# An encoder layer on one core: value product copied in halves, one filler matmul moved ahead of each head's first scores, transposes of x spread over a pass

## The chip, the cores and the metric

The kernel runs on one core of one Trainium2 chip. The metric is device time in microseconds (us) of one launch, as the median of several runs. The profile shows one execution of the same program, engine by engine: PE (matmul), PEld (PE's weight loads), DVE, ACT, POOL, and SP, which issues the DMAs.

## What is computed

One layer with two token mixers and a gated feed-forward network, for x of 1024 tokens by 1024 channels, all in float32. Branch A is the banded softmax attention, branch B the stick-breaking attention. Cut to what matters:

```python
h = x @ w_in[l]
qa, ka, va, qb, kb, vb, ga, gb = jnp.split(h, split_pts, axis=-1)
y_a = chunk_band_attention(heads_a(qa), heads_a(ka), heads_a(va), rel_bias[l]) @ w_proj_a[l]
y_b = stick_breaking_attention(heads_b(qb), heads_b(kb), heads_b(vb)) @ w_proj_b[l]
gate_a = jax.nn.sigmoid(ga + b_gate[l, :D])
gate_b = jax.nn.sigmoid(gb + b_gate[l, D:])
mix = (gate_a * y_a + gate_b * y_b) @ w_out[l]
x = layer_norm(DEEPNORM_ALPHA * x + mix, ln1_g[l], ln1_b[l])
gu = x @ w_ffn_in[l]
g, u = jnp.split(gu, 2, axis=-1)
ffn = (jax.nn.silu(g) * u) @ w_ffn_out[l]
x = layer_norm(DEEPNORM_ALPHA * x + ffn, ln2_g[l], ln2_b[l])
# chunk_band_attention, per head of 64 channels; a query sees its own chunk of 64 tokens and the 8 before it
scores = q @ k.T / 8 + rel_bias[clip(distance)];  out = softmax(scores) @ v
```

Each branch has eight heads of 64 channels.

## The kernel before

Every float32 product is made from two parts per operand: a rounded high part (fp32r) that ACT casts, and the rest, which DVE gets by subtracting (`split`). A product is then three matmuls (high·high, high·low, low·high), or two where the second operand is stacked on the partitions. The program runs as stages in this order: input projections, the attention of branch A (eight heads), that of branch B (eight heads), branch projections and gates, the output projection with the first layer norm, the feed-forward network. Some large products use a seven-product scheme on quarters of the matrices (`pair_steps`); the steps here do not need it.

**A head of branch A.** Queries come in eight blocks of 128 (b = 0 to 7). `soft_block` makes one block: two or four matmuls into a PSUM bank with the tag "sc" (L695, L696), DVE's custom instruction L738 that adds the bias and takes a running minimum into `st`, ACT's exponential L744, DVE's reciprocal and POOL's scaling L749. `value_steps` then works in two groups g of four query blocks (512 columns). For each block of keys kb, `turn` transposes the weights on PE (L807, into a bank with the tag "tr") and splits them into `pt` (ACT cast L110, DVE subtraction L111); `mult` adds two matmuls, high and low part (L820, L821), into one PSUM bank `pv` of 512 columns. There is one such bank. The order of key blocks is 4, 5, 6, 7, 3, 2, 1, 0 in the first group (g = 0) and 7, 6, 5, 4 in the second (g = 1). In the first group kb = 1 touches columns 0 to 255 and kb = 0 columns 0 to 127 alone; in the second, kb = 5 and kb = 4 do the same. After the last pair ACT copies the bank's 512 columns to `yt` or `yv` (L839), a DMA moves half of the rows, and POOL adds (L843).

**Fillers.** PE is given other matmuls between those of a head: the products of the gates (`gps`, L598), three for each of eight weight blocks, and later those of the first projection. A counter `goal` rises with each step of a head and `fill_until(goal)` takes matmuls from the generator until the counter is met.

**The order around the change.** The loop at the end of the attention part is a list of 12 steps per head. `LEAD` says how many blocks of scores are issued by each step; at the step with position 2 the first block of the *next* head is issued (`LEAD[0][2]` is 9, one more than a head's eight). `pend` holds products back by `LAG` = 2 steps. A scheduler then orders each engine's instructions by priority and data; the rows under "The change" show what comes out.

**The output projection.** It has eight tiles of 128 tokens (`tt`); tiles 4 to 7 are made in plain form, in two passes, hf = 0 for the columns 0 to 511 and hf = 1 for the columns 512 to 1023, 24 matmuls per tile and pass (`ops`, L117, L118, L120). DVE adds each to `acc` (`take_in`, L1322); in the second pass `norm_1` follows for each tile. The feed-forward network wants the normed x transposed: `x1_operands(0, ...)` transposes tiles 0 to 3 (already normed) in pairs kt, kt + 4 (four transposes each, L1178, into "tr" banks), splits each into `x1A` (ACT cast, DVE subtraction) and keeps an unsplit copy `x1raw` (ACT, L1188). There are three "tr" banks. All four pairs are issued after tile 4 of the second pass.

Of the kernel before, what the change touches and what calls it, by code (L numbers as in the profile page):

```python
# [18 lines left out]
P = 128  # L19
# [11 lines left out]
HW = 512  # L31
# [17 lines left out]
def hybrid_trunk_kernel(ctx: ExitStack, tc, x, xt, w_first, w_v, w_in, b_gate, rel_bias, w_proj,  # L49
# [6 lines left out]
    nc = tc.nc  # L56
# [7 lines left out]
    def slot(tag, name, dtype=F32):  # L64
        return pool.tile([P, 1024], dtype, tag=tag, name=name, bufs=SLOTS[tag])
# [16 lines left out]
    mm = nc.tensor.matmul  # L82
# [208 lines left out]
    for j in range(4):  # L291
        cs = (LO, HI)[j % 2]
# [495 lines left out]
    def value_steps(hd, g, wt):  # L788

        br, h = hd["br"], hd["h"]  # L790
        reach = (4, 8)[br]
        q0 = 4 * g
        nm = f"{'ab'[br]}{hd['n']}_{g}"
        pv = []

        kbs = [4, 5, 6, 7, 3, 2, 1, 0] if g == 0 else [7, 6, 5, 4]
        steps = []
        for i, kb in enumerate(kbs):
            lo_q = max(q0, kb - reach)
            hi_q = min(q0 + 3, kb)  # L800
            n = (hi_q - lo_q + 1) * P
            pts = []

            def turn(kb=kb, lo_q=lo_q, hi_q=hi_q, n=n, pts=pts):
                tp = bank("tr", f"tp_{nm}_{kb}")
                for qb in range(lo_q, hi_q + 1):
                    tr(tp[:, (qb - lo_q) * P:(qb - lo_q + 1) * P],  # L807
                       wt[qb - q0][:, (kb - qb) * P:(kb - qb + 1) * P], ident)
                pt = slot("pt", f"pt_{nm}_{kb}", F32R)
                split(pt[:, 0:n], pt[:, HW:HW + n], tp[:, 0:n])  # L810
                pts.append(pt)

            def mult(i=i, kb=kb, lo_q=lo_q, n=n, pts=pts):
                v = hd["v"]
                if i == 0:
                    pv.append(bank("pv", f"pv_{nm}"))
                last = i == len(kbs) - 1
                cs = slice((lo_q - q0) * P, (lo_q - q0) * P + n)
                pt = pts[0]
                mm(pv[0][:, cs], v[:, kb, :], pt[:, 0:n], start=(i == 0), stop=False)  # L820
                mm(pv[0][:, cs], v[:, kb, :], pt[:, HW:HW + n], start=False, stop=last)  # L821
                if last:
                    yt = hd["yt"]()
                    r = slice(h * DH, (h + 1) * DH)
                    gs = slice(g * HW, (g + 1) * HW)
                    if hd["i"] == 7:
                        nc.scalar.copy(yt[r, gs], pv[0][DH:P])
                        nc.vector.tensor_tensor(yt[r, gs], pv[0][0:DH], yt[r, gs], ALU.add)
                        if h == 1:
                            if g == 0:  # L830
                                yh[7], yl[7] = (slot("xt", f"y{p}7", F32R) for p in "hl")
                            split(yh[7][:, gs], yl[7][:, gs], yt[:, gs])
                    else:

                        if g == 0:
                            hd["yv"] = slot("yt", f"yv_{nm}")
                        yv = hd["yv"]
                        both, other = (yt, yv) if h == 0 else (yv, yt)
                        nc.scalar.copy(both[:, gs], pv[0])  # L839
                        dma(other[r, gs], both[(DH, 0)[h]:(P, DH)[h], gs])  # L840

                        def add():
                            nc.gpsimd.tensor_tensor(yt[r, gs], yt[r, gs], yv[r, gs], ALU.add)  # L843
                            if h == 1 and g == 1:
                                if hd["i"] > 4:
                                    for n, cs in ((6, LO), (8, HI)):
                                        later.append([n, lambda cs=cs: split_y(hd["i"], yt, cs)])
                                else:
                                    dma(y_dr[hd["i"]], yt)
                        later.append([3 + hd["br"], add])  # L850

            steps.append((turn, mult))
        return steps

# [96 lines left out]
    def fill_until(t):  # L951
        while state["t"] < t and not state["done"]:
            try:
                state["t"] += next(fill)
            except StopIteration:
                state["done"] = True
# [44 lines left out]
    goal = 0.0  # L1001
# [4 lines left out]
    for si, (hd, g, st, box) in enumerate(vsteps):  # L1006
        hidx, pos = si // nhead, si % nhead
# [13 lines left out]
        early = hd["br"] == 0 and st == LAG - 1 and len(pend) == LAG  # L1021
        if early and g == 1:
            pend.pop(0)()
        while wi < min(hidx * 8 + LEAD[hd["br"]][pos], len(wunits)):
            wunits[wi]()
            wi += 1
# [13 lines left out]
        last = goal  # L1040
# [18 lines left out]
    acc_t = []  # L1059
# [38 lines left out]
    for n, c in enumerate((6, 7, 5, 4, 2, 3, 1, 0)):  # L1098
# [25 lines left out]
        else:  # L1124
            g = m_first[c - 4]
# [42 lines left out]
    ops_1 = {p: [] for p in range(1, 8)}  # L1168
    x1raw, x1low, ops_21 = [], [], []

    def x1_operands(hf, acc_t):

        for kt in range(4):
            tps = []
            for k in (kt, kt + 4):
                tp = bank("tr", f"x1ps{hf}_{k}")
# [50 lines left out]
    def left_f(f):  # L1227
        prep_left(Wf[f], f"f{f}", w_ffn_in[f], "bw" if f == 2 else "op")
# [139 lines left out]
    for hf, cs in enumerate((LO, HI)):  # L1368
        for tt in range(4, 8):
# [17 lines left out]
                    right_f(1)  # L1387
            if hf == 1:
                norm_1(tt)
                if tt == 4:  # L1390
                    x1_operands(0, acc_t)
        if hf == 0:
            left_f(2)

    first_h = []

# [177 lines left out]
```

## Time and profile before

| what | us |
|---|---|
| runs of the kernel before | 1424.55, 1424.86, 1427.96 (median 1424.86) |
| the profiled execution, own time | 1425.8 |
| its span | 1424.0 |
| branch A's attention in the trace | about 342.5 to 475 |
| one of its heads | about 15.7 |
| output projection's plain tiles | about 735 to 775 |

The profiled execution took 1425.8 us by its own time, 0.9 us more than the median of the runs, and its span is 1.8 us shorter than that. The trace gives for every instruction its start, its length and, where its engine was idle ahead of it, the idle time with the event that ended it. Matmuls overlap one another in the records, so on PE the distance from start to start counts and not the length. PEld rows are weight loads; a wait of a matmul for data shows there first.

### The profile page before, as it was taken

The numbers are of one execution on the slowest core, as the hardware profiler recorded it, in microseconds if no ns is written. First come the engines' busy times: TensorE is split into PE (matmuls) and PEld (weight loads), VectorE is DVE, ScalarE is ACT, GpSimd is POOL, SyncE is SP. The second block draws the span as 40 slices with busy tenths as digits, with TensorE's granted clock in tenths as the row PEclk, the third lists the DMA queues.
The fourth block names the chain that finished last, engine by engine and source line by source line (L and its number), as shares of the span: only waits on it lengthen the run. The fifth ranks groups of instructions, "written<-read, shape, count | busy, mean of one in ns | idle before, by whom it ended". The sixth has DMA issues, their size and how long they took to land.

```text
span 1424.0 us, 19039 instructions
## 1 busy us (share of the span) xinstructions
PE 1412.3 (99%) x6672; PEld 1172.8 (82%) x6672; DVE 1054.5 (74%) x1669; ACT 683.0 (48%) x1188; POOL 245.9 (17%) x313
## 2 busy tenths in 40 slices
PE   9999999999999999999999999999999999999997
PEld 7888888888888888888888888888888888888886
DVE  8866657635777778878988947776777656978767
ACT  6444444555778788774423624444444433212201
POOL 0000000002555779750001000000000000100014
PEclk9999999999999999999999999999999999999999
DMA  7486478856676468755651224443444458787602
GB/s 255 159 295 223 163 251 311 294 183 212 213 222 199 135 228 296 249 196 198 231 198 69 74 75 163 148 148 135 150 159 163 148 192 280 281 312 238 204 15 104
DMA packets 104974, 276.54 MB, mean 194 GB/s; under 512 B 10400, under 2 KB 26784, under 8 KB 104880
## 3 DMA queue, kind: packets, MB, share of 16 engines
q1 hardware_dynamic: 104880, 275.35, 55.9%
q8 instruction: 52, 0.85, 0.3%
q14 instruction: 42, 0.34, 0.1%
HBM read 179.33 MB, written 92.30 MB: 191 GB/s over the span
## 4 chain that ended last, share of the span: by engine, by line
PE 93%; DVE 4%; ACT 2%; issue 1%; DMA 0%; POOL 0%; DVEq 0%; ACTq 0%; SPq 0%
PE sxf L180 16%; PE sxp L180 9%; PE szf L180 8%; PE dx L1496 6%; PE v L482 5%; PE szp L180 5%; PE gps L598 4%; PE syf L180 4%; PE dz L1496 3%; PE yAps L896 3%; PE syp L180 2%; PE tp_b L807 2%; PE ops L1343 2%; PE tp_a L807 2%; PE plain L348 2%; PE fpswh_h L118 2%
## 5 line engine op out<-in xcount | busy, mean ns | idle before, releaser
L784 POOL TENSOR_TENSOR w_b<-w_b,kp_b 128x511 f32<-128x511 f32 (+3 forms) x96 | 96.1, 1017 | 24.9 <-DVE kp_b L779 17.1
L1452 POOL TENSOR_TENSOR wdyt<-wdyt 128x512 f32<-128x512 f32 x8 | 11.2, 1405 | 512.5 <-DVE wdgt L1451 492.0
L779 DVE TENSOR_TENSOR_SCAN kp_b<-kp_b,ident_ps 128x512 f32<-128x512 f32 (+2 forms) x64 | 56.5, 884 | 23.3 <-ACT kp_b L776 22.4
L776 ACT ACTIVATE kp_b<-sc_b 128x512 f32<-128x512 f32 (+3 forms) x96 | 48.4, 505 | 30.7 <-PE sc_b L696 27.4
L180 PE MATMUL szf<-x1S63h,wcf 128*128 128x512 f32 x168 | 55.1, 389 | 0.0
L111 DVE TENSOR_TENSOR pt_b<-tp_b,pt_b 128x512 fp32r<-128x512 f32 (+1 forms) x96 | 50.0, 544 | 6.9 <-ACT pt_b L110 6.3
L719 POOL MEMSET bias<- 64x64 f32 x2 | 0.3, 144 | 313.4 <-ACT bias L715 313.4
L1427 DVE TENSOR_TENSOR x<-dx,x 128x512 f32<-128x512 f32 x64 | 43.3, 685 | 14.7 <-PE dx L1496 14.6
L111 DVE TENSOR_TENSOR sl<-h,sl 128x512 fp32r<-128x512 f32 x56 | 38.3, 685 | 19.5 <-ACT sl L110 19.5
L749 POOL TENSOR_SCALAR w_a<-w_a,st_a 128x640 f32<-128x640 f32 (+2 forms) x64 | 42.3, 666 | 57.3 <-PE sc_a L696 23.8
L110 ACT CAST sl<-h 128x512 fp32r<-128x512 f32 x56 | 34.7, 619 | 35.3 <-PE syf L180 17.1
L110 ACT CAST pt_b<-tp_b 128x512 fp32r<-128x512 f32 (+1 forms) x96 | 47.5, 505 | 8.0 <-PE tp_b L807 7.6
L744 ACT ACTIVATE w_a<-w_a,st_a 128x640 f32<-128x640 f32 (+2 forms) x64 | 44.8, 702 | 13.5 <-DVE st_a L738 12.2
L1156 POOL TENSOR_TENSOR mv<-mv,neghalf 128x1 f32<-128x1 f32 x16 | 11.9, 744 | 222.1 <-DVE mv L1155 222.0
L1274 ACT ACTIVATE h<-sxf 128x512 f32<-128x512 f32 x21 | 12.5, 597 | 77.3 <-PE sxf L180 77.3
L777 ACT ACTIVATE w_b<-sc_b 128x511 f32<-128x511 f32 (+3 forms) x96 | 48.6, 506 | 0.0
L111 DVE TENSOR_TENSOR pt_a<-tp_a,pt_a 128x512 fp32r<-128x512 f32 (+1 forms) x96 | 44.9, 485 | 4.8 <-ACT pt_a L110 3.1
L807 PE MATMUL tp_b<-ident,w_b 128*128 128x128 f32 x288 | 47.8, 273 | 0.4 <-DVE pt_b L111 0.3
L110 ACT CAST pt_a<-tp_a 128x512 fp32r<-128x512 f32 (+1 forms) x96 | 39.1, 432 | 11.0 <-PE tp_a L807 10.8
L807 PE MATMUL tp_a<-ident,w_a 128*128 128x128 f32 x240 | 43.2, 275 | 1.0 <-POOL w_a L749 0.4
L807 PEld LDWEIGHTS tp_b<-ident,w_b 128*128 128x128 f32 x288 | 35.6, 140 | 9.6 <-PE sc_b L696 1.3
L598 PE MATMUL gps<-xl,wh_g 128*128 128x512 f32 x96 | 43.0, 448 | 0.0
(1787 smaller groups left out, 4814.3 us busy)
## 6 DMA issues: line engine op xcount, KB each, us to landing
s_dr<-sl SPq DMA_DIRECT2D x112, 256.0 KB, 2.3
sd<-s_dr SPq DMA_DIRECT2D x56, 512.0 KB, 4.7
wLf<-in_w_ffn_in_dram SPq DMA_DIRECT2D x22, 512.0 KB, 4.5
wRf<-in_w_ffn_in_dram SPq DMA_DIRECT2D x22, 512.0 KB, 3.6
v_dr<-vc SPq DMA_DIRECT2D x16, 512.0 KB, 3.2
qs<-q_dr SPq DMA_DIRECT2D x16, 512.0 KB, 6.9
kh<-k_dr SPq DMA_DIRECT2D x16, 512.0 KB, 6.1
kl<-k_dr SPq DMA_DIRECT2D x16, 512.0 KB, 6.9
```

The lines of the kernel that those rows point to most:

```text
L110: return (nc.scalar.copy(dst_h, src), nc.vector.tensor_tensor(dst_l, src, dst_h.bitcast(F32), ALU.subtract))
L111: nc.vector.tensor_tensor(dst_l, src, dst_h.bitcast(F32), ALU.subtract))
L180: mm(acc, lw[:, ks], rx, start=(first and kt == i == 0), stop=(kt == 3 and i == 2), skip_group_check=not first)
L482: mm(accs[j], a, b, start=(first and kt == n == 0), stop=(kt == 3 and n == 2), skip_group_check=True)
L598: mm(acc[hf], lw[:, ks], rx[k][:, (LO, HI)[hf]], start=(k == j == 0), stop=(k == KT - 1 and j == 2))
L744: nc.scalar.activation(s[:, 0:w], s[:, 0:w], AF.Exp, bias=st[:, m:m + 1], scale=-1.0, accum_out=st[:, 2:3])
L776: nc.scalar.activation(kp[:, c0:e], sc[:, 0:n], AF.Sigmoid, scale=-1.0)
L777: nc.scalar.activation(be[:, m0:e], sc[:, m0 - c0:n], AF.Sigmoid)
L779: nc.vector.tensor_tensor_scan(kp[:, 0:e], kp[:, 0:e], ident_ps()[:, 0:e], 0.0, ALU.mult, ALU.add)
L784: nc.gpsimd.tensor_tensor(be[:, m0:e], be[:, m0:e], kp[:, m0 - 1:e - 1], ALU.mult)
L807: tr(tp[:, (qb - lo_q) * P:(qb - lo_q + 1) * P], wt[qb - q0][:, (kb - qb) * P:(kb - qb + 1) * P], ident)
L1496: mm(acc, a, b, start=(first and i == n == 0), stop=(i == n - 1 == 1), skip_group_check=not first)
```

## The change

It has three parts.

First, in branch A the bank `pv` is copied in two pieces. The columns 256 to 511 are copied after the pair that precedes the last two (kb = 2 in the first group, kb = 6 in the second), and the columns 0 to 255 after the last pair. The tile `yv` is taken at the first copy.

Second, at position 2 of a step list of branch A, `fill_until(goal + 0.5)` takes one filler before the scores of that step are issued.

Third, `x1_operands(0, ...)` takes a list of pairs: pair 0 is issued after the first pass (after `left_f(2)`), pairs 1 and 2 after tile 4 of the second pass, and pair 3 after tile 5.

```diff
+        def copy_out(part):
+            yt = hd["yt"]()
+            if "yv" not in hd:
+                hd["yv"] = slot("yt", f"yv_{nm}")
+            both, other = (yt, hd["yv"]) if h == 0 else (hd["yv"], yt)
+            nc.scalar.copy(both[:, g * HW:(g + 1) * HW][:, part], pv[0][:, part])
+            return both, other
...
-                mm(pv[0][:, cs], v[:, kb, :], pt[:, 0:n], start=(i == 0), stop=False)
-                mm(pv[0][:, cs], v[:, kb, :], pt[:, HW:HW + n], start=False, stop=last)
+                two = br == 0
+                done = two and i == len(kbs) - 3
+                mm(pv[0][:, cs], v[:, kb, :], pt[:, 0:n], start=(i == 0), stop=False,
+                   skip_group_check=two)
+                mm(pv[0][:, cs], v[:, kb, :], pt[:, HW:HW + n], start=False, stop=last or done,
+                   skip_group_check=two)
+                if done:
+                    copy_out(slice(2 * P, HW))
...
-                        if g == 0:
-                            hd["yv"] = slot("yt", f"yv_{nm}")
+                        both, other = copy_out(slice(0, 2 * P if two else HW))
                         yv = hd["yv"]
-                        both, other = (yt, yv) if h == 0 else (yv, yt)
-                        nc.scalar.copy(both[:, gs], pv[0])
...
+        if hd["br"] == 0 and pos == 2:
+            fill_until(goal + 0.5)
         while wi < min(hidx * 8 + LEAD[hd["br"]][pos], len(wunits)):
...
-    def x1_operands(hf, acc_t):
+    def x1_operands(hf, acc_t, kts=range(4)):
-        for kt in range(4):
+        for kt in kts:
...
                 norm_1(tt)
-                if tt == 4:
-                    x1_operands(0, acc_t)
+                if tt < 6:
+                    x1_operands(0, acc_t, ((1, 2), (3,))[tt - 4])
         if hf == 0:
             left_f(2)
+            x1_operands(0, acc_t, (0,))
```

The number of matmuls is the same; ACT has 16 instructions more (two copies of 256 columns for each one of 512). In the changed file L807 becomes L815, L820 and L821 become L830 and L832, the copy is L801, L1178 becomes L1191 and L1188 becomes L1201.

On ACT, in the third head of branch A from the cast of key block 0 of its first group to the exponential of block 5 (w_a and st_a: a block's weights and sums; pt_a_0_x and pt_a_1_x: split weights of key block x in group 0 and 1; bias: the next heads' bias tile), there stands before:

```order
L110 CAST pt_a_0_0_3397<-tp_a_0_0_3395 128x128
L110 CAST pt_a_1_7_3428<-tp_a_1_7_3423 128x512
L744 ACTIVATE w_a_0_3_3297,st_a_3_3411<-w_a_0_3_3297,st_a_3_3411 128x640
L839 COPY yt_3437<-pv_a_0_3330 128x512
L110 CAST pt_a_1_6_3445<-tp_a_1_6_3441 128x384
L110 CAST pt_a_1_5_3466<-tp_a_1_5_3463 128x256
L744 ACTIVATE w_a_1_0_3449,st_a_4_3451<-w_a_1_0_3449,st_a_4_3451 128x512
L715 ACTIVATE bias_3459<-braw_3409 128x640
L110 CAST pt_a_1_4_3474<-tp_a_1_4_3472 128x128
```

and with the change

```order
L110 CAST pt_a_0_0_3401<-tp_a_0_0_3399 128x128
L801 COPY yt_3407<-pv_a_0_3334 128x256
L110 CAST pt_a_1_7_3435<-tp_a_1_7_3430 128x512
L744 ACTIVATE w_a_0_3_3302,st_a_3_3418<-w_a_0_3_3302,st_a_3_3418 128x640
L801 COPY yt_3407<-pv_a_0_3334 128x256
L110 CAST pt_a_1_6_3450<-tp_a_1_6_3446 128x384
L110 CAST pt_a_1_5_3471<-tp_a_1_5_3468 128x256
L110 CAST pt_a_1_4_3479<-tp_a_1_4_3477 128x128
L744 ACTIVATE w_a_1_0_3454,st_a_4_3456<-w_a_1_0_3454,st_a_4_3456 128x512
L715 ACTIVATE bias_3464<-braw_3416 128x640
L801 COPY yt_3407<-pv_a_1_3483 128x256
```

One copy of the first group now stands behind the cast of key block 0 and one where the whole copy stood; the first copy of the second group stands behind an exponential and the bias, and the cast of key block 4 ahead of these two.

On PE, in the first group of the same head, its last two products with the semaphores that each waits for, before:

```order
L820 MATMUL pv_a_0_3330<-pt_a_0_1_3388,v_3100 128x256 [waits Activation_49]
L821 MATMUL pv_a_0_3330<-pt_a_0_1_3388,v_3100 128x256 [waits DVE_49]
L598 MATMUL gps_0_3322<-xh_251,wh_g_3000 128x512
L820 MATMUL pv_a_0_3330<-pt_a_0_0_3397,v_3100 128x128 [waits Activation_49]
L821 MATMUL pv_a_0_3330<-pt_a_0_0_3397,v_3100 128x128 [waits DVE_49]
```

and with the change

```order
L830 MATMUL pv_a_0_3334<-pt_a_0_1_3392,v_3102 128x256 [waits Activation_49]
L832 MATMUL pv_a_0_3334<-pt_a_0_1_3392,v_3102 128x256 [waits DVE_49]
L598 MATMUL gps_0_3326<-xh_251,wh_g_3001 128x512
L830 MATMUL pv_a_0_3334<-pt_a_0_0_3401,v_3102 128x128
L832 MATMUL pv_a_0_3334<-pt_a_0_0_3401,v_3102 128x128 [waits DVE_49]
```

The order is the same; the product of key block 0 has lost its own wait for ACT, since the one of key block 1 ahead of it now waits for a later instruction of ACT, the copy of the columns 256 to 511.

On PE, at the end of that head and the start of the next (sc_a_0: first scores of the next head; tp_a_0_x: its own block's or the next head's transposes), before:

```order
L820 MATMUL pv_a_1_3478<-pt_a_1_4_3474,v_3100 128x128
L821 MATMUL pv_a_1_3478<-pt_a_1_4_3474,v_3100 128x128
L695 MATMUL sc_a_0_0_3536<-kh_3405,qs_3403 128x320
L696 MATMUL sc_a_0_0_3536<-kl_3407,qs_3403 128x320
L695 MATMUL sc_a_0_1_3540<-kh_3405,qs_3403 128x320
L696 MATMUL sc_a_0_1_3540<-kl_3407,qs_3403 128x320
L807 MATMUL tp_a_0_6_3547<-ident,w_a_0_2_3296 128x128
L807 MATMUL tp_a_0_6_3547<-ident,w_a_0_3_3297 128x128
L598 MATMUL gps_0_3322<-xh_255,wl_g_3001 128x512
L598 MATMUL gps_0_3322<-xh_257,wh_g_3000 128x512
```

and with the change

```order
L830 MATMUL pv_a_1_3483<-pt_a_1_4_3479,v_3102 128x128
L832 MATMUL pv_a_1_3483<-pt_a_1_4_3479,v_3102 128x128
L598 MATMUL gps_0_3326<-xh_255,wl_g_3002 128x512
L695 MATMUL sc_a_0_0_3543<-kh_3412,qs_3410 128x320
L696 MATMUL sc_a_0_0_3543<-kl_3414,qs_3410 128x320
L695 MATMUL sc_a_0_1_3547<-kh_3412,qs_3410 128x320
L696 MATMUL sc_a_0_1_3547<-kl_3414,qs_3410 128x320
L815 MATMUL tp_a_0_6_3554<-ident,w_a_0_2_3301 128x128
L815 MATMUL tp_a_0_6_3554<-ident,w_a_0_3_3302 128x128
L598 MATMUL gps_0_3326<-xh_257,wh_g_3001 128x512
```

One filler has moved from behind the scores and two transposes to ahead of them. Likewise the product of key block 5 in the second group now stands behind one filler more.

The transposes of x on PE go in these runs (own count of the rows; "ops" are matmuls of the second pass): before 24 ops of tile 4, x1ps 0, 4, 1, then 6 ops, x1ps 5, 6 ops, x1ps 2, 6, 6 ops, x1ps 3, 6 ops, x1ps 7; with the change x1ps 0, 4, then 24 ops of tile 4, x1ps 1, 5, 2, then 8 ops, x1ps 6, 16 ops, x1ps 3, 7. On DVE the subtractions for x1ps 0 and 4 move ahead of two layer-norm statistics and of tile 4's `take_in`.

## The prediction

> **What bounds the kernel now.** First the page's first part and its chain of work.
>
> ```profile
> span 1424.0 us, 19039 instructions
> PE 1412.3 (99%) x6672; PEld 1172.8 (82%) x6672; DVE 1054.5 (74%) x1669; ACT 683.0 (48%) x1188; POOL 245.9 (17%) x313
> ...
> PE 93%; DVE 4%; ACT 2%; issue 1%; DMA 0%; POOL 0%; DVEq 0%; ACTq 0%; SPq 0%
> ```
>
> PE is busy in 99% of the span and makes 93% of the chain. The number of matmuls stays as it is, so only the gaps between them can change the time, and 99% says that they are few. All that the change can win or lose lies in two stretches, the attention of branch A and the last pass of the output projection. The view by stages (columns: stretch, its length, busy time of PE, PEld, DVE, ACT and POOL with counts, granted PE clock, DMA share, GB/s) shows the first, beside a part of the feed-forward network:
>
> ```profile
> 342.50:475.00 132.50, 131.02 (x791) 111.33 (x789) 102.81 (x350) 106.43 (x273) 76.78 (x99) 1.00 0.64 193
> 800.00:1100.00 300.00, 300.00 (x1324) 248.08 (x1323) 210.41 (x287) 129.12 (x192) 0.00 (x0) 1.00 0.41 142
> ```
>
> The clock is full in both, and later PE has no gap at all. In branch A ACT is busy 106.43 of 132.50 us, 80%, against 43% later: here a wait for ACT can come about, and ACT work that is added or put in another place is not free. The waits of the weight loads there (engine, tile, line; what was waited for; us in total, times, longest):
>
> ```profile
> PEld pv_a L820 <- ACT yt L839: 1.3, 4, 0.5
> PEld pv_a L820 <- ACT yv_a L839: 0.9, 3, 0.3
> ```
>
> Both rows are the first product of a group waiting for the copy that empties the one pv bank: 1.3 + 0.9 = 2.2 us in 7 places, one at each step from a head of branch A to the next. What a place costs PE, and what follows it, is read from single instructions.
>
> **Part 1a, the wait that the halves shorten.** The start of a head, PE (distances from start to start count), the weight load, and ACT:
>
> ```profile
> 388.04 0.27 PE L821 MATMUL pv_a<-pt_a,v 128*128 128x128 f32 x1
> 388.26 0.42 PE L695 MATMUL sc_a<-kh,qs 128*128 128x320 f32 x1
> 388.52 0.31 PE L696 MATMUL sc_a<-kl,qs 128*128 128x320 f32 x1
> 388.67 0.31 PE L695 MATMUL sc_a<-kh,qs 128*128 128x320 f32 x1
> ...
> 389.68 0.47 PE L598 MATMUL gps<-xl,wh_g 128*128 128x512 f32 x1
> 390.13 0.50 PE L820 MATMUL pv_a<-pt_a,v 128*128 128x512 f32 x1
> 390.47 0.39 PE L821 MATMUL pv_a<-pt_a,v 128*128 128x512 f32 x1
> 390.70 0.34 PE L820 MATMUL pv_a<-pt_a,v 128*128 128x384 f32 x1
> ```
> ```profile
> 390.13 0.19 PEld L820 LDWEIGHTS pv_a<-pt_a,v 128*128 128x128 f32 x1 [0.28 <-ACT yt L839]
> ```
> ```profile
> 389.50 0.58 ACT L839 COPY yt<-pv_a 128x512 f32<-128x512 f32 x1
> ```
>
> An undisturbed matmul of 512 columns costs 390.70 - 390.47 = 0.23 us. From the filler at 389.68 to the product at 390.13 are 0.45, so 0.22 are lost; from there to 390.47 are 0.34, another 0.11. The copy ends at 390.08 and the load starts 0.05 later: the copy is what is waited for. 0.33 in 7 places are 2.3, which agrees with the 2.2 of the waits. How long does a copy of 256 columns take? The trace has none; the nearest rows, by shape, on ACT in branch A:
>
> ```profile
> L110 ACT CAST pt_a<-tp_a 128x256 fp32r<-128x256 f32 x24 | 9.2, 382 | 2.2 <-PE tp_a L807 2.1
> L839 ACT COPY yv_a<-pv_a 128x512 f32<-128x512 f32 x8 | 4.7, 589 | 0.1
> L839 ACT COPY yt<-pv_a 128x512 f32<-128x512 f32 x8 | 4.6, 578 | 0.0
> ```
>
> I take 0.38, the cast of that shape from the same kind of bank (bounds: 0.29, half of a copy, and 0.58, no saving). The last copy then ends 0.20 earlier, 389.88, about when PE is ready. Two 0.38 for one 0.58 add 0.18 of ACT work 16 times, 2.9 us; it lies beside PE unless a copy is waited for (1c).
>
> **Part 1b and 2, the filler ahead of the scores.** In the same rows the first scores start 0.22 after the product of 128 columns, and the second 0.26 after the first; the later pair shows 0.15 for 320 columns (388.67 - 388.52), and I take 0.10 for 128, as for the transposes of 128 in part 3. So 0.12 + 0.11 = 0.23 are lost, 7 heads give 1.6 us. What is waited for stands on DVE:
>
> ```profile
> 388.13 0.08 DVE L738 DVE_READ_ACCUMULATOR2_ANT st_a<- 128x1 f32 x1
> ```
>
> It ends at 388.21 and frees the bank for the scores at 388.26. A filler of 0.23 put ahead covers 0.23. But then PE comes about 0.2 sooner to the product at 390.13, while the copy that it waits for hangs on DVE and ACT, not on PE's filler. So the two gains are not simply added: together 0.56 per boundary are lost now, 0.43 can go (0.23 by the filler, 0.20 by the shorter copy), and about 0.05 of that is late again elsewhere. I take 0.37 × 7 = 2.6 us, and 0.3 more for the step into branch B, which has the same scores-after-product order (an estimate from the 0.23 above). Bounds: 0, if DVE or the copy is as late as before relative to PE, and 0.56 × 8 = 4.5.
>
> **Part 1c, the wait that the halves bring.** The rows of PE's order show that the product of key block 1 now waits for a later ACT instruction than its own cast, and that the product behind it has lost its wait: the half copy, which reads columns that this product does not touch, is put ahead of it because both use one bank. So the first half is not copied beside the last two products; they stand behind it. First group of the same head, ACT and then PE:
>
> ```profile
> 380.42 0.83 ACT L744 ACTIVATE w_a<-w_a,st_a 128x640 f32<-128x640 f32 x1 [1.03 <-DVE st_a L738]
> ...
> 381.25 0.24 ACT L110 CAST pt_a<-tp_a 128x128 fp32r<-128x128 f32 x1
> ```
> ```profile
> 381.33 0.48 PE L598 MATMUL gps<-xh,wl_g 128*128 128x512 f32 x1
> 381.65 0.28 PE L820 MATMUL pv_a<-pt_a,v 128*128 128x256 f32 x1
> ```
>
> The half copy stands behind the cast that ends at 381.49; it ends at 381.49 + 0.38 = 381.87, and with the 0.05 above the product can go at 381.92 instead of 381.65: 0.27 us, and all that PE does later queues behind it. In the fourth head the new order puts a filler and a transpose ahead of that product, 0.33, which covers the wait; the seven others give 1.9 us. Bounds per place: 0, if ACT is earlier against PE there, and 0.62 (0.24 for a whole cast, 0.38 for the copy).
>
> In the second group the half copy stands behind the cast of key block 4, an exponential and the bias:
>
> ```profile
> 384.72 0.74 ACT L744 ACTIVATE w_a<-w_a,st_a 128x512 f32<-128x512 f32 x1
> ...
> 385.44 0.74 ACT L715 ACTIVATE bias<-braw 128x640 f32<-128x640 f32 x1
> 386.06 0.27 ACT L110 CAST pt_a<-tp_a 128x128 fp32r<-128x128 f32 x1
> ```
> ```profile
> 386.52 0.28 PE L820 MATMUL pv_a<-pt_a,v 128*128 128x256 f32 x1
> ```
>
> The exponential's start moves back by the cast, 0.2; the bias follows 0.72 and the copy 0.62 behind (385.44 - 384.72, 386.06 - 385.44), so the copy runs from 386.26 to 386.64 and the product may go at 386.69. PE has put one filler of 0.23 ahead, its turn is 386.75: nothing is lost, by 0.06. I take 0.05 in seven heads, 0.3. In the first head the order also puts a weight cast of 1024 columns there:
>
> ```profile
> 354.81 1.06 ACT L549 CAST wh_g<-wr_g 128x1024 fp32r<-128x1024 f32 x1
> ```
>
> It stood behind the products before and stands ahead of the half copy now: 1.06 less what PE can do meanwhile. I take 0.8 (bounds 0 and 1.06). Losses: 1.9 + 0.3 + 0.8 = 3.0 us. Some of it is not seen in the end, since a PE that comes later to the boundary behind it waits less there: I take 0.3 off, 2.7.
>
> Why a copy of other columns stands ahead of a product at all can be weighed by a row of part 3: ACT waits 0.90 us for DVE's reading of the very bank that it is to read itself. The Trainium skill, "PSUM — Partial Sum Buffer", section "PSUM bank collisions raise a hardware error", has the rule: guard by bank and quadrant of partitions, not by address, since two engines on disjoint columns of one bank collide too. It speaks against this part of the change: by it the waits stay and cost the 3.0; by addresses alone they would cost nothing. The 0.90 and the waits in the order agree with it.
>
> **Part 3, the transposes.** Tile 4's stretch: the waits, then PE, ACT and DVE:
>
> ```profile
> PEld x1ps L1178 <- ACT x1raw L1188: 1.9, 4, 1.3
> ```
> ```profile
> 754.33 0.40 PE L120 MATMUL ops<-wh_o,mo 128*128 128x512 f32 x1
> 755.59 0.66 PE L1178 MATMUL x1ps<-ident,acc 128*128 128x128 f32 x4 [0.87 <-ACT x1raw L1188]
> 756.00 0.49 PE L117 MATMUL ops<-wh_o,mo 128*128 128x512 f32 x1
> ```
> ```profile
> 754.95 0.58 ACT L1188 COPY x1raw<-x1ps 128x512 f32<-128x512 f32 x1 [0.90 <-DVE x1A L111]
> ```
> ```profile
> 753.05 0.68 DVE L1152 BATCH_NORM_STATS2 bn<-acc 128x6 f32<-128x512 f32 x1
> 753.65 0.67 DVE L1322 SCALAR_TENSOR_TENSOR acc<-acc,ops 128x512 f32<-128x512 f32 x1
> 754.24 0.68 DVE L111 TENSOR_TENSOR x1A<-x1ps,x1A 128x512 fp32r<-128x512 f32 x1
> ...
> 756.15 0.63 DVE L111 TENSOR_TENSOR x1A<-x1ps,x1A 128x512 fp32r<-128x512 f32 x1
> ```
>
> 755.59 - 754.33 - 0.23 = 1.03 us are lost: x1ps 5 needs the bank of x1ps 0, which ACT's copy gives back, which waits for DVE's subtraction, which stands behind statistics and the `take_in`. With pair 0 ahead of the pass that wait goes. The next one is x1ps 6, which needs the bank of x1ps 1. PE comes to it after eight transposes and two matmuls more than it had done at 754.56 (754.33 + 0.23); four transposes take 0.41 (756.00 - 755.59), so at 754.56 + 0.82 + 0.46 = 755.84. DVE's subtraction of x1ps 1 has one statistic less ahead, 0.60 (753.65 - 753.05): it ends at 756.78 - 0.60 = 756.18, and the copy of 0.58 at 756.76. 0.9 is lost again, a gain of 0.1. The three smaller waits of the first row, 1.9 - 1.3 = 0.6 on the loads, partly go with the 16 matmuls that now stand ahead of x1ps 3: 0.2. I take 0.3 (bounds: 1.03 + 0.6 gained; 0.6 lost, if the subtraction comes one place later).
>
> **The sum.** -2.6 - 0.3 + 2.7 - 0.3 = -0.5 us. Against the profiled execution's own time (span 1424.0, own time 1.8 more: 1425.8) that is 1425.3; the median of the runs shown is 0.94 lower, 1424.86, and the same difference there gives **1424.4 us**.
>
> **The rivals.** *The new wait is hidden*: ACT has the casts of key blocks 0 and 4 done before PE's turn, so that the half copies end in time. For it speaks the 0.06 of the second group; against it, ACT's 80%. Without the losses of 2.7 the sum is -3.2, 1421.7; with the bounds of all gains (4.5 + 1.6) it is -6.1, 1418.8. *The new wait is dearer than its removal is worth*: in all 16 places (a first and a second group in eight heads) PE's turn comes when the cast ahead of the half copy has only begun, 0.24 + 0.38 = 0.62 each, 9.9 us; less gains of 3.2 gives +6.7, 1431.6. It decides from 3.2 / 16 = 0.20 us a place on, and it is slower by more than 0.3% from (3.2 + 4.3) / 16 = 0.47. For it: the exponential ahead already waits 1.03 for DVE, so ACT is late there by data and not by load; against it: 0.27 and 0.0 in the head worked out. *The change does nothing at the boundary*: the scores and the product wait for DVE and ACT at the same instants whatever PE does before them, while the new waits stay; then +2.7 - 0.3 = +2.4, 1427.3.
>
> **How the numbers follow.** 0.3% of 1424.86 is 4.3 us, about what a measurement here can tell from no change: faster is below 1420.6, slower above 1429.1. Forecast (1422.5 to 1426): 0.52. Hidden wait: 0.25, from 1421.7 down to 1418.8 by how much of the bounds is reached, 0.15 of it below 1420.6. Nothing gained at the boundary: 0.13, all within. Dearer wait: 0.10, of it 0.08 above 1429.1. So faster 0.15, same 0.77, slower 0.08. The range leaves 0.1 at either end: from 1420.2, short of the bound of all gains (1418.8), to 1428.3, past the case without gain.
>
> **What would show it.** In the changed profile: waits of the weight loads of L830 for the copies L801 at key blocks 1 and 5, about 0.27 in first groups and near 0 in second ones, against fewer at the first product of a group (from 2.2 us to under 1); no wait of sc_a at a head's start; ACT's copies of 256 columns near 0.38; x1ps 5 without a wait and x1ps 6 with one near 0.9; span near 1423.5. I would be wrong if the half copies show no wait on PE, if a wait above 0.5 stands at them, or if a difference arose outside the two stretches.

## The result and the profile after

The changed kernel takes 1427.83 us (median of 20 runs, 1426.89 to 1430.58) against 1425.68 us before (median of 20 runs, 1424.55 to 1427.96). The ratio is 1.0014 with a 95% interval of 1.0008 to 1.0021: slower by 2.15 us, about 1.1 to 3.0. The forecast was 0.5 us faster; the sign was wrong. The page's head for the changed kernel:

```profile
span 1425.3 us, 19055 instructions
## 1 busy us (share of the span) xinstructions
PE 1411.3 (99%) x6672; PEld 1171.9 (82%) x6672; DVE 1054.2 (74%) x1669; ACT 685.4 (48%) x1204; POOL 244.7 (17%) x313
```

ACT has the 16 instructions more and 2.4 us more work; PE is busy 1.0 us less in a span that is 1.3 us longer. So the time is in waits of PE. The weight loads' waits in branch A (340 to 478 us; engine, tile, line; what was waited for; us in total, times, longest):

```profile
PEld pv_a L830 <- ACT yt L801: 3.7, 7, 1.1
PEld pv_a L830 <- ACT yv_a L801: 2.8, 6, 0.8
PEld sc_a L695 <- DVE st_a L738: 1.9, 4, 0.5
PEld tp_a L815 <- DVE pt_a L111: 1.0, 2, 0.7
...
PEld pv_a L832 <- DVE pt_a L111: 0.3, 1, 0.3
```

Waits for a copy have grown from 2.2 us in 7 places to 6.5 in 13: six at key block 1, six at key block 5, one at a head's first product. The waits of the low-part products for DVE, 2.6 us in 10 places before, have almost gone. These are idle times of the weight loads and PE does not lose all of each, so I worked out what PE loses by place. For every product, score and transpose in branch A I took the distance from the start of the matmul ahead to its own start, less the shortest distance for a matmul of the shape ahead (0.226 us for 512 columns, 0.175 for 384, 0.146 for 320, 0.118 for 256, 0.105 for 128, 0.090 for a transpose), and summed over the eight heads, from the first value product to the last. A constant part of up to 0.1 us per instruction is in each, so only differences between kernels count. A row for a key block is its two matmuls, high and low part.

| place, us | before | changed | whole copy, filler moved | half copy ahead |
|---|---|---|---|---|
| scores | 3.28 | 3.25 | 2.13 | 1.41 |
| first product of a head (two matmuls) | 2.34 | 0.92 | 3.43 | 2.42 |
| key block 1, first group | 0.65 | 2.03 | 0.65 | 2.36 |
| key block 5, second group | 0.66 | 4.02 | 0.65 | 0.80 |
| all other products | 4.34 | 2.95 | 4.24 | 2.94 |
| transposes | 5.32 | 5.80 | 5.69 | 5.89 |
| fillers, scores of B, rest | -2.28 | -2.70 | -2.96 | -3.09 |
| sum | 14.31 | 16.29 | 13.83 | 12.72 |

The third and fourth columns are the first and sixth experiments. Key block 5 alone lost 3.4 us, more than the whole change. The place in the third head, in the changed kernel: ACT, then DVE, then PE.

```profile
384.08 0.18 ACT L744 ACTIVATION_READ_ACCUMULATOR w_a<-w_a,st_a 128x1 f32 x1
384.17 0.35 ACT L801 COPY yt<-pv_a 128x256 f32<-128x256 f32 x1
384.42 1.07 ACT L110 CAST pt_a<-tp_a 128x384 fp32r<-128x384 f32 x3
386.13 0.72 ACT L744 ACTIVATE w_a<-w_a,st_a 128x512 f32<-128x512 f32 x1 [0.64 <-DVE st_a L738]
...
386.85 0.72 ACT L715 ACTIVATE bias<-braw 128x640 f32<-128x640 f32 x1
387.48 0.35 ACT L801 COPY yt<-pv_a 128x256 f32<-128x256 f32 x1
```
```profile
384.29 0.16 DVE L748 RECIPROCAL st_a<-st_a 128x1 f32<-128x1 f32 x1 [0.45 <-ACT w_a L744]
384.93 0.56 DVE L111 TENSOR_TENSOR pt_a<-tp_a,pt_a 128x384 fp32r<-128x384 f32 x1 [0.48 <-ACT pt_a L110]
385.41 0.68 DVE L738 CUSTOM_DVE_ANT_0 w_a<-sc_a,bias 128x512 f32<-128x512 f32 x1
386.01 0.08 DVE L738 DVE_READ_ACCUMULATOR2_ANT st_a<- 128x1 f32 x1
```
```profile
387.06 0.40 PE L598 MATMUL gps<-xh,wh_g 128*128 128x512 f32 x1
387.89 0.38 PE L830 MATMUL pv_a<-pt_a,v 128*128 128x256 f32 x1 [0.43 <-ACT yt L801]
388.11 0.28 PE L832 MATMUL pv_a<-pt_a,v 128*128 128x256 f32 x1
```

Read it from the bottom. The product of key block 5 waits for the half copy that ends at 387.83. The copy stands behind the bias (386.85), that behind the exponential of block 4 (386.13), and the exponential waited 0.64 for DVE. DVE did its bias instruction for block 4 (the 128x512 row of L738) at 385.41, behind the subtraction of key block 6 (the 128x384 row of L111), which itself waited 0.48 for ACT's cast. Before, DVE did those two the other way round:

```profile
383.87 0.69 DVE L738 CUSTOM_DVE_ANT_0 w_a<-sc_a,bias 128x512 f32<-128x512 f32 x1
384.48 0.08 DVE L738 DVE_READ_ACCUMULATOR2_ANT st_a<- 128x1 f32 x1
384.60 0.89 DVE L111 TENSOR_TENSOR pt_a<-tp_a,pt_a 128x384 fp32r<-128x384 f32 x2
```

and the exponential could start at 384.72. This swap is in six of the heads; the fourth head has DVE's old order, and there the wait at key block 5 does not exist (0.095 us from the table's method, as without any copy, against 0.58 to 0.81 in heads 1, 2, 3, 5 and 6). Head 7 has the swap and loses only 0.09 us more than before: there no bias instruction stands between the exponential and the half copy on ACT. In head 1 the swap is not what delays the copy, since the exponential waits for nothing that the profile shows; the weight cast of 1024 columns, which stood behind the exponential before, is ahead of it:

```profile
353.27 1.08 ACT L549 CAST wh_g<-wr_g 128x1024 fp32r<-128x1024 f32 x1
354.22 0.75 ACT L744 ACTIVATE w_a<-w_a,st_a 128x512 f32<-128x512 f32 x1
```

In the output projection the waits of x1ps for x1raw went from 1.9 us to

```profile
PEld x1ps L1191 <- ACT x1raw L1201: 0.7, 1, 0.7
```

By the distances on PE a loss of 1.04 us became one of 0.49, at x1ps 6, as the new order said.

### The profile page after: what moved, and what is told of

The parts are those of the page before. It is cut to its first block, busy times and chain, and to the rows that moved or that the text cites. A ratio compares the mean times of both kernels' runs of the same rounds, so it can differ in the third digit from the quotient of the medians.

```text
span 1425.3 us, 19055 instructions
## 1 busy us (share of the span) xinstructions
PE 1411.3 (99%) x6672; PEld 1171.9 (82%) x6672; DVE 1054.2 (74%) x1669; ACT 685.4 (48%) x1204; POOL 244.7 (17%) x313
## 4 chain that ended last, share of the span: by engine, by line
PE 89%; DVE 5%; ACT 2%; DMA 2%; issue 1%; POOL 1%; DVEq 0%; ACTq 0%; POOLq 0%; SPq 0%
PE sxf L180 16%; PE sxp L180 9%; PE szf L180 8%; PE dx L1510 6%; PE v L482 5%; PE szp L180 4%; PE syf L180 4%; PE gps L598 3%; PE dz L1510 3%; PE yAps L907 3%; PE syp L180 2%; PE tp_b L815 2%; PE ops L1356 2%; PE plain L348 2%; PE fpswh_h L120 2%; PE fpswh_h L117 2%
## 5 line engine op out<-in xcount | busy, mean ns | idle before, releaser
L111 DVE TENSOR_TENSOR pt_b<-tp_b,pt_b 128x512 fp32r<-128x512 f32 (+1 forms) x96 | 50.0, 544 | 6.8 <-ACT pt_b L110 6.2
L111 DVE TENSOR_TENSOR sl<-h,sl 128x512 fp32r<-128x512 f32 x56 | 38.4, 686 | 20.6 <-ACT sl L110 20.6
L111 DVE TENSOR_TENSOR pt_a<-tp_a,pt_a 128x512 fp32r<-128x512 f32 (+1 forms) x96 | 45.5, 486 | 8.0 <-ACT pt_a L110 7.3
L815 PE MATMUL tp_b<-ident,w_b 128*128 128x128 f32 x288 | 47.8, 273 | 0.4 <-DVE pt_b L111 0.3
L815 PE MATMUL tp_a<-ident,w_a 128*128 128x128 f32 x240 | 43.5, 275 | 1.1 <-DVE pt_a L111 0.6
L815 PEld LDWEIGHTS tp_b<-ident,w_b 128*128 128x128 f32 x288 | 35.6, 140 | 9.6 <-PE sc_b L696 1.3
```

The source lines that it names most:

```text
L111: nc.vector.tensor_tensor(dst_l, src, dst_h.bitcast(F32), ALU.subtract))
L815: tr(tp[:, (qb - lo_q) * P:(qb - lo_q + 1) * P], wt[qb - q0][:, (kb - qb) * P:(kb - qb + 1) * P], ident)
```

## The experiments

**Theories.** The *queue theory*: the loss is at the half copies, which the products of the same bank wait for, and it is large only in the second group because there the copy stands behind an exponential that DVE's new order makes late. The *split theory*: every split bank costs its part, wherever the copy stands. The *filler theory*: the moved filler is what costs. The *load theory*: 16 more copies make ACT late.

Times are medians of 11 runs; before was run beside them (1425.6 to 1426.3 us), and ratios are to it. The intervals are about 0.09% either way, 1.3 us, so the places on PE decide and the times go beside them. The sums by place repeat well: the first and the eighth experiment have the same branch A and give 3.43 and 3.43, 0.65 and 0.64, 2.13 and 2.10; the transposes do not (5.69 and 6.52). The stretch from first scores to last value product repeats less well (139.74 and 140.91 for these two), so differences under 1 us in it say nothing.

### e1: the whole copy back

```diff
-                two = br == 0
+                two = False
```

> The changed kernel with the whole copy back (two = False): filler and transposes as changed. Halves theory: the new waits at key blocks 1 and 5 go (about 4.7 us on PE), the wait of the first product of a head for the whole copy comes back (about 1.4): about 1424.5 us, 3 us under the changed kernel and about 1 us under before. Filler theory (the moved filler is what costs): still 1427 or more.

Measured: 1425.57 us, ratio 0.9996 (0.9987 to 1.0005). Key blocks 1 and 5 are back at 0.65 each; the first product is at 3.43. The filler theory falls: with the filler moved the loss is gone. The time is 1.1 us above what was expected.

### e2 and e3: halves in one group only

```diff
-                two = br == 0
+                two = br == 0 and g == 0
```

(and `g == 1` in e3)

> Changed kernel, but halves only in the first group. DVE's bias instruction of block 4 still stands behind the subtraction of key block 6, yet no half copy is queued behind the exponential that waits for it. Queue theory: no wait at key block 5, about 1.4 us at key block 1 stay, boundary wait of 2 us back in part: about 1425.8. Split theory (every split bank costs its part, wherever the copy stands): half of the loss stays, about 1426.7. If the DVE order costs by itself, 1427.5.

> Changed kernel, but halves only in the second group. DVE's order is that of before, so the exponential of block 4 is on time; the half copy stands behind one cast more. Queue theory: 0.2 to 0.4 us lost per head at key block 5 in place of 0.6 to 0.8, nothing at key block 1: about 1425.2. Split theory: the loss at key block 5 stays at about 4 us in all, 1426.4.

Measured: e2 1426.81 us, ratio 1.0004 (0.9996 to 1.0013); e3 1426.69 us, 1.0005 (0.9996 to 1.0014). In e2, DVE has its new order in the same six heads, yet key block 5 is at 0.65: DVE's order by itself costs nothing there. Key block 1 is at 2.38 and the first product at 3.54. In e3 DVE has its old order and key block 5 is at 2.65 in place of 4.02, 0.23 in each of the second, third and sixth heads where the changed kernel has 0.58 to 0.60. The places are those of the queue theory; the times are nearer to those of the split theory, since I had expected the first product's wait to come back less in e2 and key block 5 to fall further in e3. Summed over all places, e2 is 1.1 us above e1 and e3 is 1.1 above it, and the changed kernel, with both, 2.5: that too is what the split theory would give. These two alone did not decide. They show one thing more: the swap on DVE comes with the halves of the first group (e2 has it, e3 does not), and it is the half copy of the second group that it makes late.

### e4: block 4 issued one step sooner

```diff
-LEAD = ((6, 8, 9, 9, 10, 10, 11, 11, 12, 12, 13, 13),
+LEAD = ((6, 8, 9, 9, 10, 10, 11, 11, 12, 13, 13, 13),
```

> Changed kernel with the step list's tenth entry 13 in place of 12: the next head's block 4 of scores is issued one step sooner, DVE has its bias instruction ahead of the subtraction of key block 6 again, ACT has bias and exponential ahead of the cast of key block 5. Both halves stay. Queue theory: the wait at key block 5 falls from about 0.6 to under 0.2 us a head, 2.5 us less, about 1425.3. Split theory: as the changed kernel, 1427.8 within 0.5.

Measured: 1425.22 us, ratio 0.9993 (0.9984 to 1.0002). Both halves are still there. Key block 5 went to 2.07 in all: no wait in the second, third, fourth and sixth heads, 0.58 and 0.63 in the first and fifth. It speaks for the queue theory, but this edit moves rows on PE and ACT too.

### e5: DVE's order alone undone

```diff
+            tc.add_manual_dep(turned[hd["n"]].ins, scored.ins.name, ...)
```

The edge puts the subtraction of key block 6 behind the bias instruction of block 4.

> The changed kernel with one edge more: DVE's subtraction of key block 6 has to stand behind the bias instruction of block 4, as in the kernel before. ACT's order then has the cast of key block 4 again between the bias and the half copy. Queue theory: the exponential of block 4 starts about 1 us sooner against PE, the half copy about 0.7 sooner (one cast more ahead of it), so that 0.2 to 0.3 us a head are lost at key block 5 in place of 0.7: branch A's stretch (first scores to last value product, 142.3 in the changed kernel) falls by 1.2 to 2 us. Split theory: 142.3 within 0.3.

Measured: 1426.1 us, ratio 0.9999 (0.9990 to 1.0008). Key block 5 fell from 4.02 to 2.21. In the third head, ACT and PE:

```profile
385.38 0.72 ACT L748 ACTIVATE w_a<-w_a,st_a 128x512 f32<-128x512 f32 x1
...
386.10 0.72 ACT L715 ACTIVATE bias<-braw 128x640 f32<-128x640 f32 x1
386.73 0.25 ACT L110 CAST pt_a<-tp_a 128x128 fp32r<-128x128 f32 x1
386.87 0.37 ACT L805 COPY yt<-pv_a 128x256 f32<-128x256 f32 x1
```
```profile
386.89 0.48 PE L598 MATMUL gps<-xh,wl_g 128*128 128x512 f32 x1
387.30 0.38 PE L836 MATMUL pv_a<-pt_a,v 128*128 128x256 f32 x1
```

The exponential waits for nothing now, and the copy ends at 387.24 with the product 0.06 behind: 0.41 us after the filler ahead of it, against 0.83 in the changed kernel (387.06 to 387.89). The rest of the wait is the queue of exponential, bias and cast. The second, third and sixth heads went from about 0.6 to under 0.2, the fifth from 0.81 to 0.31. The first head stayed at 0.65: its queue on ACT has the weight cast in it here too. The edit does not leave the other engines as they were: ACT has the cast of key block 4 between the bias and the half copy, and in the second, third and sixth heads PE has one filler less ahead of the product.

### e6 and e7: the half copy put ahead on ACT

```diff
+                    if g == 1 and hd["n"] + 1 in turned:
+                        tc.add_manual_dep(turned[hd["n"] + 1].ins, hd["copied"].ins.name, ...)
+                    if g == 0 and "cast0" in hd:
+                        tc.add_manual_dep(hd["cast0"].ins, hd["copied"].ins.name, ...)
```

The first edge (e6) puts the exponential of block 4 behind the half copy; DVE keeps its new order. The second (e7 has both) puts the cast of key block 0 behind the first group's half copy.

> The changed kernel with one edge more: ACT's exponential of block 4 has to stand behind the half copy of the second group. Only that copy moves on ACT, ahead of the exponential and the bias; DVE's order stays as changed. Queue theory: the wait at key block 5 goes, about 3.3 us less in branch A's stretch (139 in place of 142.3), and about 1424.5 us for the kernel. Split theory: the product of key block 5 is behind the copy anyway, half of the loss stays, 141. If the exponential is now late for something else, it shows as waits of transposes on POOL's scaling.

> As the kernel with the copy ahead of the exponential, and in the first group the half copy ahead of the cast of key block 0 too. Queue theory: the wait at key block 1 falls from 0.2 by most of a cast's 0.2 us a head, another 0.7 to 1.2 us: branch A's stretch about 138, the kernel about 1423.5. Split theory: no change from the kernel with the first edge alone, or the cast of key block 0 is late in its turn and the product of key block 0 waits.

Measured: e6 1424.59 us, ratio 0.9990 (0.9982 to 0.9999); e7 1424.49 us, 0.9989 (0.9980 to 0.9998). In e6 key block 5 is at 0.80 and the stretch of branch A at 138.63 us. ACT and PE in the third head:

```profile
385.97 0.37 ACT L805 COPY yt<-pv_a 128x256 f32<-128x256 f32 x1 [0.75 <-PE pv_a L836]
386.24 0.73 ACT L745 ACTIVATE w_a<-w_a,st_a 128x512 f32<-128x512 f32 x1
```
```profile
386.49 0.48 PE L598 MATMUL gps<-xh,wl_g 128*128 128x512 f32 x1
386.80 0.28 PE L834 MATMUL pv_a<-pt_a,v 128*128 128x256 f32 x1
```

The copy starts as soon as PE's product of key block 6 is done, after 0.75 us in which ACT was idle, and it ends at 386.34, 0.46 ahead of the product. The exponential comes behind it, some 0.35 us later than it could have started by DVE (whose instruction ended at 385.84); no loss at a value product shows for that. On ACT the edit puts the half copy ahead of the exponential and the bias; on PE the product of key block 5 stands one filler sooner again in most heads, where it stood before, so PE even wants the copy sooner. DVE keeps the swap. With both halves kept the whole loss at key block 5 is gone (0.14 above an undisturbed product is left, in the first head): the split theory falls for the second group, and it is the copy's place in ACT's queue that sets the loss. In e7 key block 1 went from 2.36 to 1.52, as expected, but the time shows nothing of it within its interval.

### e8: the filler alone

```diff
+        if hd["br"] == 0 and pos == 2:
+            fill_until(goal + 0.5)
```

> The kernel before with the moved filler alone. The waits of a head's first scores for DVE (1.6 us) go, but PE comes 0.2 us sooner to the wait for the whole copy: 0.4 to 0.6 us won in branch A's stretch (140.2 before). If the two gains added up as separate, 1.6.

Measured: 1426.52 us, ratio 1.0004 (0.9995 to 1.0013). The scores went from 3.28 to 2.10, 1.2 us less, and the first product from 2.34 to 3.43, 1.1 more. The waits:

```profile
PEld pv_a L820 <- ACT yt L839: 1.9, 4, 0.7
...
PEld pv_a L820 <- ACT yv_a L839: 1.4, 3, 0.5
```

What PE no longer loses at the scores, it loses less than 2 us later at ACT's copy: the loads wait 3.3 us for it in place of 2.2. The filler alone shows no gain.

### e9 and e10: the last copy put ahead too

```diff
+                        if two and g == 1 and turned["five"][0] == hd["n"] + 1:
+                            tc.add_manual_dep(turned["five"][1].ins, hd["copied"].ins.name, ...)
```

The edge puts the cast of the next head's key block 5 behind the last half copy; e9 has all three edges, e10 the first and third and halves in the second group alone.

> As the kernel with two edges, and the last half copy of the second group stands ahead of the cast of the next head's key block 5 on ACT. Queue theory: what is left of the wait at a head's first product (1.2 us over the heads above an undisturbed matmul, and 0.5 at the matmul behind) goes, since that cast takes 0.46 and the wait is 0.2 to 0.3 a head; the product of key block 5 is then just in time. About 1 to 1.5 us less, 1423.2. Rival: the product of key block 5 now waits for its late cast and nothing is won, 1424.5.

> Halves in the second group alone, with the two edges of that group (half copy ahead of the exponential, last copy ahead of the cast). Queue theory: the wait at key block 1 (1.4 us of PE) is gone too, that at key block 5 stays at none: about 1423, and the best of all. Rival: the exponential, on time there before, is now held behind the half copy, and what needs its result is late: 1424.5 or more.

Measured: e9 1424.27 us, ratio 0.9990 (0.9981 to 0.9999); e10 1424.67 us, 0.9993 (0.9985 to 1.0002). The first product fell to 0.69 in both, as the queue theory has it, but the time did not follow. In e10 the waits of branch A now begin with

```profile
PEld pv_a L838 <- DVE pt_a L111: 4.7, 15, 0.5
```

Of these, 2.6 us in 10 places were there in the kernel before. The rest is new: the cast comes later, so DVE's subtraction behind it does, and the low part of the product waits for that (1.1 us at key block 5 of the first group in e9 and 1.08 in e10, 0.0 before). The rival had the cast in mind; it is the subtraction behind it. These do not beat e6.

### e11: both half copies at the end

```diff
-                done = two and i == len(kbs) - 3
+                done = False
...
-                if done:
+                if two and last:
                     copy_out(slice(2 * P, HW))
```

> The changed kernel with both half copies after the last pair: ACT has its 16 copies more, and no product of the same group stands behind a copy. Load theory (16 copies more make ACT late): the wait at a head's first product grows from 3.4 us (whole copy with the filler moved) by 0.18 a head to about 4.6, nothing else; about 1426.5. Queue theory says the same of this place and no wait at key blocks 1 and 5; if waits show there, neither holds.

Measured: 1426.36 us, ratio 1.0003 (0.9994 to 1.0011). First product 3.84, against 3.43 with whole copies; key blocks 1 and 5 at 0.64 and 0.66, all other products 4.58 against 4.24. The 16 extra copies alone cost 0.4 + 0.3 us on PE, less than the 1.2 expected at the first place, and nothing at key blocks 1 and 5: the load theory does not account for the loss there.

### e12: the transposes alone

```diff
-                if tt == 4:
-                    x1_operands(0, acc_t)
+                if tt < 6:
+                    x1_operands(0, acc_t, ((1, 2), (3,))[tt - 4])
```

(with pair 0 ahead of the second pass)

> The kernel before with the transposes of x spread alone. The stretch of the output projection (first to last of its matmuls up to the first of the feed-forward, 86.43 before and 85.82 in the changed kernel) falls by 0.3 to 0.6; branch A's stretch stays as before. About 1425.5.

Measured: 1425.35 us, ratio 0.9996 (0.9987 to 1.0005). The projection's stretch was 86.27 us, against 86.43 before, 86.39 in e8, and 85.82 to 86.31 in the eleven other kernels with this part: 0.1 to 0.6 less, and 0.16 for this part alone. The plain tiles' matmuls run from 724.6 to 772.8 us in the trace of before, not from about 735 as the table of times has it. Branch A's places are as before (first product 2.34, key blocks 0.65 and 0.64).

## Why the prediction was wrong

**The step that failed** is the second group of part 1c. It said "nothing is lost, by 0.06. I take 0.05 in seven heads, 0.3", and 0.8 for the first head; 1.1 us in all. Measured are 3.4 (0.66 to 4.02): 0.65 in the first head, near the 0.8 and with the weight cast that was named in the queue, and 2.7 in the seven others in place of 0.3. The wait itself, its place and its cause (the half copy's bank) were named; the time of the copy was wrong. I put the exponential of block 4 where the trace of before had it, at 384.72 plus 0.2 for a cast, and took only ACT's new order into account. But the exponential waits for DVE, and DVE's order had changed at that place too: with the old time of DVE's instruction the sum gave a copy at 386.26, 0.49 ahead of PE's turn at 386.75. With the new order it was at 387.48, 0.19 behind PE's turn (387.06 + 0.23 = 387.29). The shift of 0.68 is about the 0.64 that the exponential waited for DVE. The fourth head (DVE as before, no wait), e5 (DVE's order put back: 4.02 to 2.21) and e6 (copy put ahead: 0.80) show it from three sides. e2 shows that DVE's order without the copy costs nothing at this place, and e3 that the copy with DVE's old order costs less (0.23 a head in place of about 0.6). The sign of being wrong that the prediction named, a wait above 0.5 at a half copy, is there.

**The first group** was right in size and wrong in its net. 1.9 us were forecast at key block 1, and 1.4 measured. But of the 0.3 us that I took off because a later PE waits less elsewhere, there were 1.4: all other products fell from 4.34 to 2.95, mostly the low parts' waits for DVE (2.6 us to 0.3). Over the value products this group cost about nothing. Over all places it did not come free: e2 is 1.1 us above e1, with 0.8 of it at scores that wait for DVE (the sum over all places is less sure than the single ones).

**The gains** were forecast as 2.6 at the heads' starts and 0.3 at the step into branch B. At these places they came: the first products gave 1.4, the scores behind a head's last product 1.2 (1.59 to 0.35), the first scores of B 0.5 (0.97 to 0.51). The count of steps was off: of the seven waits that the prediction read as one at each step, six are at the first products of heads 2 to 7 and one is in the second group of the fifth head, and six steps, not seven, have scores of branch A behind them. What the forecast lacked is a new wait of scores for DVE, behind the first products of heads 3, 4, 6 and 7 (1.9 us in 4 places; on PE 0.12 became 1.99), so that the row of the scores shows no gain (3.28 to 3.25). These are the heads that follow heads 2, 3, 5 and 6, in which the swap delays the half copy. In e2, which has the swap and no half copy in the second group, the scores wait behind the last products of heads 2, 3, 5 and 6 (1.26 us over the six steps, against 0.45 in e1); in e5 and e6 neither wait is there, and in e6 the scores gain 1.9 us in all. So the late copy is not the whole cause, since e2 has none, and DVE's new order alone is not, since e6 has it; the cause of this wait stays open. The sentence that the two gains are not simply added holds for the filler alone: by e8 its 1.2 come back as 1.1 of waiting for the whole copy. That ACT's copy of 256 columns takes 0.38 was right:

```profile
L801 ACT COPY yv_a<-pv_a 128x256 f32<-128x256 f32 x16 | 6.0, 377 | 1.3 <-PE pv_a L832 0.8 <-POOL w_b L784 0.5
L801 ACT COPY yt<-pv_a 128x256 f32<-128x256 f32 x16 | 5.9, 368 | 0.0
```

**Part 3**: x1ps 5 without a wait and x1ps 6 with one, as forecast; 0.55 us won on PE in the changed kernel's profile against 0.3. That profile is at the good end: x1ps 6 loses 0.49 there and 0.54 in e11, but 0.71 to 0.76 in the ten other kernels with this part, which leaves about the 0.3 of the forecast. That this size came right is luck: x1ps 6 was to lose 0.9, and 0.2 of the gain was to come from the three smaller waits of the loads, of which PE felt nothing before (no more than 0.02 us at any x1ps but 5).

**The sum by places**: -1.4 (first products) + 0 (scores: 1.2 won at the steps, 1.9 lost behind first products, 0.7 won elsewhere) - 0.4 (B's scores, fillers) + 1.4 + 3.4 (key blocks 1 and 5) - 1.4 (other products) + 0.5 (transposes, within what repeats badly) = about +2.0 in branch A, the table's 16.29 - 14.31; less 0.55 for part 3 gives +1.4. The two profiled spans differ by 1.3. The runs say 2.15 with an interval from 1.1 to 3.0, which holds it.

**The rivals.** The case that came is the one called "dearer wait", in a smaller form: 0.58 to 0.81 us at five of the 16 places, near the 0.62 worked out for a place, and 0.1 to 0.3 or nothing at the others. I gave it 0.10 because the head that I worked out by hand had 0.27 and 0.0. The time lies next to the 1427.3 of the rival without gain at the boundary, and that is luck: its gains at the boundary came, and the losses were larger than it had them. The rule of the Trainium skill ("PSUM — Partial Sum Buffer", section "PSUM bank collisions raise a hardware error": guard by bank, not by address) was the right one to weigh: in every kernel with an early half copy some products wait for it though its columns are not theirs, and with both copies at the end (e11) no such wait is left. What PE waits for is a semaphore that stands in the program; whether it was put there for the bank or for the tile the runs do not tell, since here a tile is a bank. Halves in two banks were not tried; the kernel's eight banks all have a use (two mm, two sc, three tr, one pv).

**A version that beats both** kernels is e6: 0.9990 of before (0.9982 to 0.9999), where the change stands at 1.0014 (1.0008 to 1.0021). The first interval ends just under 1, so that the gain over before is small and only just clear; that over the change is clear, as the two intervals do not meet. e7 and e9, which have the same edge, are no better within their intervals.

## What to carry to other kernels

When a change adds a wait for a copy, the time of that copy has to be followed through every queue ahead of it, in the new order of each engine: here ACT's new row was seen and DVE's, one step further back, was taken at its old time. An eviction is the copy that empties a bank. Splitting it helped here only with the early half ahead of the long instructions of its engine (e6); a half copy in the same bank as the products behind it was a wait of theirs, and its place in the queue was its price. A filler that hid one wait ahead of another just moved PE to the next wait sooner (e8), as that one was not shortened too.

## What the runs showed that was not expected

Copying a bank in two pieces after the last product (e11) cost PE only 0.7 us in all, though it puts 16 more copies on an engine that is 80% busy in that stretch. The same order of instructions in branch A gave stretches of 139.74 and 140.91 us in two profiles (e1 and e8), with the difference in transposes that waited for POOL (1.7 us in 4 places in e8): what one profile says of a whole stretch is no better than about 1 us here, while the losses at products and scores repeated to 0.03 us.
